# Block 2's mixer in a two-block model kernel: the convolution's projections stand between RWKV's k, r and v, the decayed keys come from the quotients, and scalings move from VectorE to ScalarE

## The chip, the core and the metric

The kernel runs on one core of one Trainium2 chip. The metric is the device time of one execution in microseconds (us). The kernel before takes 2485.76 us, the median of 3 runs (2484.92 to 2486.15).

## The reference

Two blocks run one behind the other, each two layers deep, on 256 tokens of width 1024 in float32. Block 1's layer is an attention mixer and a mixture of experts. Block 2's layer, which the change touches, is a mixer of three branches and a mixture of 32 experts:

```
p = h @ w_in                                  # retention | RWKV | convolution columns
y_ret  = retention(q, k, v, g, ...)
y_rwkv = rwkv7_time_mix(p_rwkv, ...)
y_conv = bgate * conv3(cgate * h_conv)        # three taps along the tokens
merged = sum(gates[i] * (y_i @ w_branch[i]))
x = x + gate1 * (merged @ w_o)
x = x + gate2 * hier_moe(modulate(rms_norm(x)))
```

RWKV's recurrence, for each of 8 heads of width 64 (w the decay, a a sigmoid, kh the normalized key):

```
pf = pf + mu * (prev_token(pf) - pf)          # before r, k, v, w, a, g are cut from it
w  = exp(-exp(-0.5) * sigmoid(w0 + tanh(wd) @ w_lora))
kh = kk * rsqrt(max(sum(kk * kk), 1e-12));  kk = k * k_k
kt = k * (1 + (a - 1) * k_a)
state = state * w - (state @ kh) (a * kh)^T + v kt^T
y     = state @ r
```

## The kernel before, in words

All weights stream from HBM through tiles of 2 MB that SyncE's queue loads in the order in which they are used (`Stream`, `mixer2_tiles`). In the mixer the ring "c" holds three tiles. The ring "x" opens behind the recurrence (`self.st.ring(spare_ring, ...)`), "e" behind retention's transposes (`late_ring()`), and the experts' tiles follow in the same stream as slots come free.

A projection of the mixer (`feat_proj`) makes 128 output columns of all 256 tokens: a chunk. ScalarE casts the weight chunk to `wh` (L240), VectorE makes the rest `wl = w - wh` (L244), each in two buffers, and TensorE does three matmuls for each of 8 row blocks: wh x hi (L249), wh x lo (L250), wl x hi (L251). A tile of weights is four chunks.

`mixer2` writes RWKV's work as straight code: the projections of w and a, then k (`project("k", 4)`), decay and cumulated decay `cum`, the key's norm, r, v, and then the chunk matrices. `shifted` mixes each token with the one before: one ScalarE copy with scale (L581), one VectorE operation (L582), and one for the first token alone (L584). With 64-token chunks, `e = exp(-cum)` divides the keys (`Ki`, `Bi`, the quotients) and `exp(cum)` scales r. `matrices` makes the within-chunk products, `double` inverts them in five levels, and the loop over four chunks `q` runs the recurrence. The keys are also needed as tokens (`toks`, transposed with matmuls, L927), decayed to the chunk's end: `kt * exp(cum_end - cum)` and the same for `a`.

The other branches are a generator, `dense()`: the convolution's three projections (h L639, cgate L644, bgate L656), its gates, its output branch, retention and its gates, and RWKV's output branch. `fill(n)` advances it by n pieces; it stands behind each token transpose, twice in each level of `double` and twice in each `q`, and `fill(1000)` runs the rest.

The text's order is not the order on the engines. With `schedule_with_timeline_sim=True` a planner simulates the program when it is built and puts on each engine the earliest written instruction that is ready by its own costs; on the chip each engine then works in that fixed order. `issue_after` ties an instruction behind another.

Tiles of 4 KB per partition come in tags: "s" with 8 buffers, "d" with 6, "t" with 3. The projections' PSUM tiles (tag "mm") have 4 buffers, the small products' (tag "ch") 2.

Of the kernel before, what the change touches and what calls it, by code (L numbers as in the profile page):

```python
# [10 lines left out]
F32 = mybir.dt.float32  # L11
# [3 lines left out]
AF = mybir.ActivationFunctionType  # L15
OP = mybir.AluOpType
# [92 lines left out]
def mixer2_tiles():  # L109
    cols = lambda *starts: [("w_in_2", (c, c + 512), 4096) for c in starts]  # L110

    def gate(br):
        return ([("w_gate_2", (1024 * br + 512 * c, 1024 * br + 512 * c + 512), 4096) for c in range(2)]
                + [("w_branch_2", br, 4096)])

    return ([("w_in_2", (3584, 3840), 2048)] + cols(2560, 2048, 3072, 3840, 4864, 4352) + gate(2)
            + cols(0, 512, 1024, 1536) + gate(0) + gate(1)
            + [("w_o_2", (512 * c, 512 * c + 512), 4096) for c in range(2)])

# [69 lines left out]
class Kernel:  # L189
# [344 lines left out]
    def mixer2(self, l, prm, mod, cs, nslot, hold, spare, spare_ring, late_ring, gs2, row):  # L534
        nc, tc = self.nc, self.tc
        norm1, mu = (prm[:, P2[n][0]:sum(P2[n])] for n in ("norm1", "mu"))
        cos, sin = cs
        with ExitStack() as ctx:
# [3 lines left out]
            sb = ctx.enter_context(tc.tile_pool(name="m2", bufs=1, reuse_waits="tile"))  # L542
# [35 lines left out]
            def shifted(dst, w, c, mc):  # L578
                p = fproj(w, c)
                m = work.tile([128, 256], F32, name="shm", tag="shm")  # L580
                nc.scalar.activation(m, p, AF.Copy, scale=mu[:, mc:mc + 1])  # L581
                nc.vector.scalar_tensor_tensor(dst[:, 1:], p[:, 1:], mu1[:, mc:mc + 1], m[:, :255], op0=OP.mult,  # L582
                                               op1=OP.add)
                nc.vector.tensor_scalar(dst[:, :1], p[:, :1], mu1[:, mc:mc + 1], None, op0=OP.mult)  # L584

            def head_norm(x, nh, hd, eps, tag):
                xv = x.rearrange("p t (h d) -> p t h d", h=nh)
# [47 lines left out]
            def dense():  # L635
# [13 lines left out]
                w = next_w()  # L649
                for c in range(4):  # L650
                    u = cv_[:, c]
                    nc.vector.tensor_scalar(yc[:, c], u, cvw[:, 2, c:c + 1], None, op0=OP.mult)
                    for i, d in ((1, 1), (0, 2)):
                        nc.vector.scalar_tensor_tensor(yc[:, c, d:], u[:, :256 - d], cvw[:, i, c:c + 1], yc[:, c, d:],
                                                       op0=OP.mult, op1=OP.add)
                    nc.vector.tensor_tensor(yc[:, c], yc[:, c], fproj(w, c), op=OP.mult)  # L656
                    yield
# [85 lines left out]
            def fill(n):  # L743
                for _ in range(n):
                    if gens and next(gens[0], 0) == 0:
                        gens.pop(0)
# [9 lines left out]
            def project(name, m0, tag="s"):  # L756
                dst = feat(name, tag)
                w = next_w()
                for c in range(4):
                    shifted(dst[:, c], w, c, m0 + c)  # L760
                self.st.done()
                return dst

            k_ = project("k", 4)
            wal = pv("wa_lora")
            lw, a_ = xfeat(2), feat("a")
            for c in range(4):
# [8 lines left out]
            with tc.issue_after(self.last_mm.ins):  # L776
# [3 lines left out]
                                     stop=k == 7)  # L780
                nc.vector.tensor_tensor(row, row, pw, op=OP.add)
                nc.vector.tensor_tensor(wr, wr, gs2[:, :, None].to_broadcast([128, 8, 36]), op=OP.mult)
            nc.vector.tensor_scalar(lw, lw, -math.exp(-0.5), None, op0=OP.mult)
            cum = feat("cum")
            for c in range(4):
                nc.vector.tensor_tensor_scan(cum[:, c], smask, lw[:, c], 0.0, op0=OP.mult, op1=OP.add)
            nc.vector.tensor_tensor(lw, cum, lw, op=OP.subtract)
            nc.scalar.activation(lw, lw, AF.Exp)

            kk, sq = feat("kk"), xfeat(3)  # L790
            for c in range(4):
                nc.vector.tensor_scalar(kk[:, c], k_[:, c], pv("k_k")[:, c:c + 1], None, op0=OP.mult)
            nc.scalar.activation(sq, kk, AF.Square)
            pn = ch([128, 2, 8], "pn")
            for t in range(2):
# [4 lines left out]
            nc.vector.tensor_scalar(kn, pn, 1e-12, None, op0=OP.max)  # L800
            kr = carve([128, 2, 8])
            self.rsqrt(sb, kr.rearrange("p t h -> p (t h)"), kn.rearrange("p t h -> p (t h)"), 16)
            for c in range(4):
                nc.vector.tensor_scalar(sq[:, c], a_[:, c], -1.0, pv("k_a")[:, c:c + 1], op0=OP.add, op1=OP.mult)
            nc.vector.scalar_tensor_tensor(k_, sq, 1.0, k_, op0=OP.add, op1=OP.mult)
            kt = k_
            r_ = project("r", 0)
            pk = ch([8, 2, 128], "pk")
            for t in range(2):
                nc.tensor.transpose(pk[:, t], kr[:, t], self.ident)  # L810
            v_ = project("v", 8, "t")
            krT = carve([8, 256])
            nc.vector.tensor_copy(krT, pk.rearrange("p t s -> p (t s)"))
            for c in range(4):
# [10 lines left out]
            for h in range(2):  # L825
                nc.vector.tensor_tensor(KRv[h][:, :, :, 0], by_chunk(kk, h), by_chunk(lw, h), op=OP.mult)
            e = feat("e")
            nc.scalar.activation(e, cum, AF.Exp, scale=-1.0)
            Ki, Bi = feat("Ki"), feat("Bi")
            nc.gpsimd.tensor_tensor(Bi, a_, e, op=OP.mult)  # L830
            nc.vector.tensor_tensor(Ki, kt, e, op=OP.mult)
            e = feat("e")
            nc.scalar.activation(e, cum, AF.Exp)
            for h in range(2):
                nc.vector.tensor_tensor(KRv[h][:, :, :, 1], by_chunk(r_, h), by_chunk(e, h), op=OP.mult)
            for c in range(4):
                nc.vector.scalar_tensor_tensor(r_[:, c], r_[:, c], pv("r_k")[:, c:c + 1], kt[:, c], op0=OP.mult,
                                               op1=OP.mult)
            cl = sb.tile([128, 4, 4], F32, name="cl")
            nc.vector.tensor_copy(cl, cum[:, :, 63::64])  # L840
            cum5 = cum.rearrange("p c (q s) -> p (c q) s", q=4)
            nc.vector.tensor_tensor(cum5, cl.rearrange("p c q -> p (c q)")[:, :, None].to_broadcast([128, 16, 64]), cum5,
                                    op=OP.subtract)
            nc.scalar.activation(cum, cum, AF.Exp)
            lamc = sb.tile([128, 4, 4], F32, name="lamc")
            nc.scalar.activation(lamc, cl, AF.Exp)
            nc.vector.tensor_tensor(kt, kt, cum, op=OP.mult)
            nc.vector.scalar_tensor_tensor(a_, a_, -1.0, cum, op0=OP.mult, op1=OP.mult)
            bon = feat("bon", "t")
            for c in range(4):  # L850
                p = ch([128, 256], "pbon")
# [9 lines left out]
            def matrices(ct):  # L861
                NA[ct], MB[ct] = j8(flat("NA")), j8(xslot(2 + ct))
                xy = tokm("XY")
                X[ct], Y[ct] = j8(xy[:, 0]), j8(xy[:, 1])
                for dst, kind, mask in ((NA[ct], 0, "msn"), (MB[ct], 1, "msk")):
                    for hf in range(2):
                        p = ch([128, 4, 128], "pmat")
                        for c, i in pairs:
                            q = 2 * ct + hf
                            kd = KRv[c // 2][half[i], c % 2, q].rearrange("p k s -> p (k s)")  # L870
                            nc.tensor.matmul(p[half[i], c], lhsT=(Bi, Ki)[kind][half[i], c, 64 * q:64 * q + 64], rhs=kd,
                                             start=True, stop=True)
                        nc.vector.tensor_tensor(dst[:, 4 * hf:4 * hf + 4], p,
                                                cv(mask)[:, None, :].to_broadcast([128, 4, 128]), op=OP.mult)
                p = ch([128, 8, 64], "pmat")
                for hf in range(2):
                    for c, i in pairs:
                        q = 2 * ct + hf
                        nc.tensor.matmul(p[half[i], 4 * hf + c], lhsT=KRv[c // 2][half[i], c % 2, q, 0],
                                         rhs=Bi[half[i], c, 64 * q:64 * q + 64], start=True, stop=True)  # L880
                nc.vector.tensor_tensor(X[ct], p, m8("msl"), op=OP.mult)
                na = NA[ct][:, :, :64]
                nc.vector.scalar_tensor_tensor(Y[ct], na, -1.0, m8("b1t"), op0=OP.mult, op1=OP.mult)
                nc.vector.tensor_tensor(Y[ct], Y[ct], m8("eye"), op=OP.add)
                nc.vector.scalar_tensor_tensor(X[ct], X[ct], -1.0, m8("b1l"), op0=OP.mult, op1=OP.mult)
                nc.vector.tensor_tensor(X[ct], X[ct], m8("eye"), op=OP.add)

            def mm8(p, lhs, rhs):
# [29 lines left out]
            for name, src in (("Vt", v_), ("Kt", kt), ("Bt", a_)):  # L918
                dst = tokp(name)
                toks.append(dst)  # L920
                for t in range(2):
                    p = ch([128, 2, 4, 64], "ptr")
                    for hf in range(2):
                        for c in range(4):
                            q = 2 * t + hf
                            for i in range(2):
                                nc.tensor.matmul(p[half[i], hf, c], lhsT=src[:, c, 64 * q:64 * q + 64],  # L927
                                                 rhs=self.ident[:, half[i]], start=True, stop=True)
                    nc.scalar.copy(dst[:, 2 * t:2 * t + 2], p)
                fill(1)  # L930
            Vt, Kt, Bt = toks

# [928 lines left out]
```

## Time and profile before

| | |
|---|---|
| median of 3 runs | 2485.76 us |
| profiled execution | 2488.0 us, span 2486.2 us |
| TensorE busy | 2031.0 us, 82% of the span |
| VectorE busy | 988.2 us, 40% |
| ScalarE busy | 578.9 us, 23% |
| GpSimd busy | 105.0 us, 4% |
| HBM read | 781.04 MB, 315 GB/s over the span |

Block 2's mixers run from about 854 to 1215 us and from 1672 to 2030 us, its experts behind each of them. In the profile, busy is the time in which an engine had an instruction at work; a row of a group of instructions ends with the idle time before them and what ended it. PEclk is the share of TensorE's full clock that was granted.

### The profile page before, as it was taken

How to read it: one execution, taken by the hardware profiler on the slowest of the kernel's cores; microseconds unless marked ns; L12 is line 12 of the kernel's file. 1: busy time of each engine (PE TensorE's matmuls, PEld its weight loads, DVE VectorE, ACT ScalarE, POOL GpSimd, SP SyncE). 2: the span in 40 equal slices, each digit the busy share in tenths (PEclk: the TensorE clock that was granted, in tenths of full speed). 3: DMA queues.
4: the chain of work that ended last, by engine and by line, in shares of the span. 5: the costliest groups of instructions: out<-in, count | busy, mean ns of one | idle time of the engine just before them, and what ended most of it. 6: DMA issues, size and time to landing. Idle time of an engine off the chain costs nothing. (4 is left out here: it accounts for less than half of the span.)

```text
span 2486.2 us, 46552 instructions
## 1 busy us (share of the span) xinstructions
PE 2031.0 (82%) x20511; PEld 1427.4 (57%) x20511; DVE 988.2 (40%) x2151; ACT 578.9 (23%) x1163; POOL 105.0 (4%) x118
## 2 busy tenths in 40 slices
PE   6998886998878699999886666569999988666665
PEld 5656443756545489989743333338998975333332
DVE  4334333435333576566421111137646653111112
ACT  4332111423111352244310000015224430100000
POOL 0000000001000010001000000001000110000000
PEclk9989998999999899999898888879999989888888
DMA  8576999585999732256699999992216669999997
GB/s 319 233 304 273 423 422 423 201 362 225 406 425 418 291 135 77 89 231 260 261 429 430 428 429 429 429 382 103 103 70 246 243 251 428 429 429 428 429 429 308
DMA packets 65126, 785.24 MB, mean 316 GB/s; under 512 B 8336, under 2 KB 8848, under 8 KB 14480
## 3 DMA queue, kind: packets, MB, share of 16 engines
q1 hardware_dynamic: 63616, 775.00, 75.5%
q10 hardware_dynamic: 1296, 7.11, 0.7%
q8 instruction: 167, 2.74, 0.4%
q14 instruction: 47, 0.39, 0.0%
HBM read 781.04 MB, written 1.05 MB: 315 GB/s over the span
## 5 line engine op out<-in xcount | busy, mean ns | idle before, releaser
L251 PE MATMUL pfeat<-hT,wl 128*128 128x256 f32 x928 | 268.6, 290 | 7.8 <-DVE wl L244 7.8
L249 PE MATMUL pfeat<-hT,wh 128*128 128x256 f32 x928 | 268.9, 290 | 3.3 <-ACT hf L402 1.6
L250 PE MATMUL pfeat<-hT,wh 128*128 128x256 f32 x928 | 265.6, 287 | 0.0
L240 ACT CAST wh<-wc 128x1024 fp32r<-128x1024 f32 x148 | 154.6, 1046 | 350.1 <-PE pfeat L250 240.6
L244 DVE TENSOR_TENSOR wl<-wc,wh 128x1024 fp32r<-128x1024 f32 x148 | 189.0, 1278 | 109.3 <-ACT wh L240 108.9
L1404 DVE TENSOR_TENSOR hs<-hs,pgu 128x128 f32<-128x128 f32 x96 | 27.5, 287 | 491.0 <-ACT hs L1403 490.5
L251 PEld LDWEIGHTS pfeat<-hT,wl 128*128 128x128 f32 x928 | 179.6, 194 | 16.7 <-DVE wl L244 10.0
L1512 DVE TENSOR_TENSOR Y<-pd,gate_row 32x256 f32<-32x256 f32 x256 | 107.6, 420 | 201.3 <-PE pd L1500 198.5
L1403 ACT ACTIVATE hs<-pgu 128x128 f32<-128x128 f32 x96 | 27.0, 281 | 689.9 <-PE pgu L1478 505.6
L249 PEld LDWEIGHTS pfeat<-hT,wh 128*128 128x128 f32 x928 | 179.7, 194 | 11.4 <-issue 3.3
L1390 PE MATMUL pg<-pick,H 128*128 128x128 f32 x1024 | 142.7, 296 | 46.6 <-ACT xg L1398 40.2
L250 PEld LDWEIGHTS pfeat<-hT,wh 128*128 128x128 f32 x928 | 179.6, 194 | 1.4 <-issue 0.7
L1390 PEld LDWEIGHTS pg<-pick,H 128*128 128x128 f32 x1024 | 131.8, 208 | 71.3 <-ACT xg L1398 54.9
L1453 PE MATMUL acc<-Y,P 128*128 128x512 f32 x256 | 129.3, 649 | 21.7 <-DVE Y L1509 15.6
L1509 DVE COPY Y<-pd 32x256 f32<-32x256 f32 x256 | 107.6, 420 | 92.0 <-PE pd L1500 88.8
L1478 PE MATMUL pgu<-wc,xg 128*32 128x256 f32 x1152 | 84.6, 437 | 58.0 <-DMA wc<-in_gu 57.8
L1453 PEld LDWEIGHTS acc<-Y,P 128*128 128x128 f32 x256 | 49.9, 207 | 81.9 <-issue 72.2
L1478 PEld LDWEIGHTS pgu<-wc,xg 128*32 128x32 f32 x1152 | 40.5, 121 | 98.1 <-issue 43.9
L1398 ACT ACTIVATE xg<-pg,mod,gs 128x128 f32<-128x128 f32 x120 | 45.8, 457 | 218.5 <-PE pgu L1478 171.2
L1478 PE MATMUL pgu<-wb,xg 128*32 128x256 f32 x1024 | 70.4, 416 | 22.3 <-DMA wb<-in_gu 22.3
L1472 PE MATMUL pgu<-wa,xg 128*32 128x256 f32 x704 | 80.1, 419 | 6.3 <-DMA wa<-in_gu 6.3
L250 PE MATMUL ptok<-wl,hT 128*128 128x512 f32 (+1 forms) x192 | 78.3, 408 | 1.9 <-DVE wl L289 1.9
(577 smaller groups left out, 3618.2 us busy)
## 6 DMA issues: line engine op xcount, KB each, us to landing
wb<-in_gu SPq DMA_DIRECT2D x54, 2048.0 KB, 29.6
wc<-in_gu SPq DMA_DIRECT2D x50, 2048.0 KB, 28.8
wc<-in_wm SPq DMA_DIRECT2D x36, 2048.0 KB, 8.3
wa<-in_gu SPq DMA_DIRECT2D x20, 2048.0 KB, 16.5
wc<-in_dn SPq DMA_DIRECT2D x16, 2048.0 KB, 38.9
wb<-in_dn SPq DMA_DIRECT2D x16, 2048.0 KB, 38.9
we<-in_gu SPq DMA_DIRECT2D x13, 2048.0 KB, 36.8
wf<-in_gu SPq DMA_DIRECT2D x13, 2048.0 KB, 37.0
```

The costliest lines, as they stand in the source:

```text
L240: nc.scalar.copy(hv, src)
L244: eng.tensor_tensor(lv, src, hv.bitcast(F32), op=OP.subtract)
L249: mm(p, lhsT=lhs[0], rhs=rhs[0], start=first, stop=False)
L250: mm(p, lhsT=lhs[0], rhs=rhs[1], start=False, stop=False)
L251: self.last_mm = mm(p, lhsT=lhs[1], rhs=rhs[0], start=False, stop=last)
L1390: nc.tensor.matmul(p[:, i], lhsT=self.H[:, t, 128 * k:128 * k + 128], rhs=disp[:, t], start=t == 0, stop=t == 1)
L1398: nc.scalar.activation(xg[:, k], p[:, i], AF.Identity, scale=g, bias=b)
L1453: nc.tensor.matmul(acc[2 * t + c], lhsT=P[:, t], rhs=Y[:, 512 * c:512 * c + 512], start=q == 0, stop=q == NE // 4 - 1, skip_group_check=True)
L1472: nc.tensor.matmul(pgu[r:r + 32], lhsT=xg[:, k, 32 * e:32 * e + 32], rhs=gv[ab][:, k, j], start=k == 0, stop=k == 7)
L1478: nc.tensor.matmul(pgu[32 * j:32 * j + 32], lhsT=xg[:, k, 32 * i:32 * i + 32], rhs=gv[k // 4][:, k % 4, j], start=k == 0, stop=k == 7)
L1509: nc.vector.tensor_copy(dst, src)
L1512: nc.vector.tensor_tensor(dst, src, g, op=OP.mult)
```

## The change

The text's order in RWKV's part becomes k, four pieces of `dense` (the convolution's h), w and a, the key's norm, r, four pieces (cgate), v, four pieces (bgate), and the weights are laid out in that order. VectorE's operations with a scale for each partition go to ScalarE: the first token of `shifted`, the convolution's last tap, `kk`, and `(a - 1) * k_a + 1`. The factor `-exp(-0.5)` goes into the exponentials' scale. `Bi = a * e` goes from GpSimd to VectorE. The decayed keys are `Ki * lamc` and `Bi * (-lamc)`, where `lamc` is `exp(cum)` at the chunk's end. One mask of `matrices` goes, and the keys of the last 64 tokens are no longer transposed.

```diff
-    return ([("w_in_2", (3584, 3840), 2048)] + cols(2560, 2048, 3072, 3840, 4864, 4352) + gate(2)
+    return ([("w_in_2", (3584, 3840), 2048)] + cols(2560, 3840, 2048, 4864, 3072, 4352) + gate(2)
...
-                nc.vector.tensor_scalar(dst[:, :1], p[:, :1], mu1[:, mc:mc + 1], None, op0=OP.mult)
+                nc.scalar.activation(dst[:, :1], p[:, :1], AF.Copy, scale=mu1[:, mc:mc + 1])
...
-                    nc.vector.tensor_scalar(yc[:, c], u, cvw[:, 2, c:c + 1], None, op0=OP.mult)
+                    nc.scalar.activation(yc[:, c], u, AF.Copy, scale=cvw[:, 2, c:c + 1])
...
             k_ = project("k", 4)
+            fill(4)
...
-            nc.vector.tensor_scalar(lw, lw, -math.exp(-0.5), None, op0=OP.mult)
+            rate = -math.exp(-0.5)
...
-            nc.scalar.activation(lw, lw, AF.Exp)
+            nc.scalar.activation(lw, lw, AF.Exp, scale=rate)
...
-                nc.vector.tensor_scalar(kk[:, c], k_[:, c], pv("k_k")[:, c:c + 1], None, op0=OP.mult)
+                nc.scalar.activation(kk[:, c], k_[:, c], AF.Copy, scale=pv("k_k")[:, c:c + 1])
...
+            nka = carve([128, 4])
+            nc.vector.tensor_scalar(nka, pv("k_a"), -1.0, 1.0, op0=OP.mult, op1=OP.add)
             for c in range(4):
-                nc.vector.tensor_scalar(sq[:, c], a_[:, c], -1.0, pv("k_a")[:, c:c + 1], op0=OP.add, op1=OP.mult)
-            nc.vector.scalar_tensor_tensor(k_, sq, 1.0, k_, op0=OP.add, op1=OP.mult)
+                nc.scalar.activation(sq[:, c], a_[:, c], AF.Identity, scale=pv("k_a")[:, c:c + 1], bias=nka[:, c:c + 1])
+            nc.vector.tensor_tensor(k_, sq, k_, op=OP.mult)
             kt = k_
             r_ = project("r", 0)
+            fill(4)
...
             v_ = project("v", 8, "t")
+            fill(4)
...
-            nc.gpsimd.tensor_tensor(Bi, a_, e, op=OP.mult)
+            nc.vector.tensor_tensor(Bi, a_, e, op=OP.mult)
...
-            cl = sb.tile([128, 4, 4], F32, name="cl")
-            nc.vector.tensor_copy(cl, cum[:, :, 63::64])
-            cum5 = cum.rearrange("p c (q s) -> p (c q) s", q=4)
-            nc.vector.tensor_tensor(cum5, cl.rearrange("p c q -> p (c q)")[:, :, None].to_broadcast([128, 16, 64]), cum5,
-                                    op=OP.subtract)
-            nc.scalar.activation(cum, cum, AF.Exp)
-            lamc = sb.tile([128, 4, 4], F32, name="lamc")
-            nc.scalar.activation(lamc, cl, AF.Exp)
-            nc.vector.tensor_tensor(kt, kt, cum, op=OP.mult)
-            nc.vector.scalar_tensor_tensor(a_, a_, -1.0, cum, op0=OP.mult, op1=OP.mult)
+            lamc, nlam = (sb.tile([128, 4, 4], F32, name=n) for n in ("lamc", "nlam"))
+            nc.vector.tensor_copy(lamc, e[:, :, 63::64])
+            nc.vector.tensor_scalar(nlam, lamc, -1.0, None, op0=OP.mult)
+            for dst, src, lam in ((kt, Ki, lamc), (a_, Bi, nlam)):
+                dst, src = (x.rearrange("p c (q s) -> p (c q) s", q=4) for x in (dst, src))
+                nc.vector.tensor_tensor(dst, src, lam.rearrange("p c q -> p (c q)")[:, :, None].to_broadcast([128, 16, 64]),
+                                        op=OP.mult)
...
-                nc.vector.tensor_tensor(X[ct], p, m8("msl"), op=OP.mult)
...
-                nc.vector.scalar_tensor_tensor(X[ct], X[ct], -1.0, m8("b1l"), op0=OP.mult, op1=OP.mult)
+                nc.vector.scalar_tensor_tensor(X[ct], p, -1.0, m8("b1l"), op0=OP.mult, op1=OP.mult)
...
-                        for c in range(4):
-                            q = 2 * t + hf
+                        q = 2 * t + hf
+                        for c in range(4 if q < 3 or src is v_ else 0):
...
-                    nc.scalar.copy(dst[:, 2 * t:2 * t + 2], p)
+                    n = 2 if not t or src is v_ else 1
+                    nc.scalar.copy(dst[:, 2 * t:2 * t + n], p[:, :n])
```

## Rows read from the trace of the kernel before

**Rows 1.** Busy time by stretch: start:end, length, engines' busy us, PEclk, DMA share, GB/s.
```profile
885.06:934.05 48.99, 46.09 (x367) 42.24 (x367) 42.22 (x70) 23.90 (x32) 9.06 (x3) 1.00 0.35 130
934.05:1019.96 85.91, 85.91 (x1613) 81.08 (x1612) 53.61 (x79) 20.79 (x27) 0.00 (x0) 1.00 0.21 76
1019.96:1051.00 31.04, 31.04 (x545) 28.90 (x545) 13.78 (x23) 8.03 (x12) 2.08 (x2) 1.00 0.20 70
1190.00:1243.00 53.00, 45.57 (x362) 36.96 (x360) 24.40 (x70) 16.24 (x28) 1.85 (x2) 0.87 0.69 266
1243.00:1675.00 432.00, 290.59 (x3279) 155.25 (x3278) 88.79 (x236) 41.24 (x111) 5.43 (x10) 0.86 1.00 424
2050.00:2486.00 436.00, 289.18 (x3353) 153.62 (x3345) 84.87 (x225) 35.35 (x100) 5.02 (x8) 0.87 0.97 412
```

**Rows 2.** TensorE's matmuls in order of time: start, length, instruction, [idle before <- releaser].
```profile
917.30 0.39 PE L251 MATMUL pfeat<-hT,wl 128*128 128x256 f32 x1 [1.28 <-DVE wl L244]
921.79 0.39 PE L251 MATMUL pfeat<-hT,wl 128*128 128x256 f32 x1 [1.35 <-DVE wl L244]
926.06 0.39 PE L251 MATMUL pfeat<-hT,wl 128*128 128x256 f32 x1 [0.27 <-DVE wl L244]
...
1735.46 0.39 PE L251 MATMUL pfeat<-hT,wl 128*128 128x256 f32 x1 [1.36 <-DVE wl L244]
```

**Rows 3.** VectorE and GpSimd in order of time, around those waits.
```profile
913.32 2.84 POOL L821 TENSOR_TENSOR a<-a,kk 128x1024 f32<-128x1024 f32 x1 [15.91 <-DVE kk L820]
916.24 3.28 POOL L830 TENSOR_TENSOR Bi<-a,e 128x1024 f32<-128x1024 f32 x1
...
913.82 3.43 DVE L244 TENSOR_TENSOR wl<-wc,wh 128x1024 fp32r<-128x1024 f32 x1
917.69 2.90 DVE L831 TENSOR_TENSOR Ki<-k,e 128x1024 f32<-128x1024 f32 x1
```

**Rows 4.** Transposes of the keys, in order of time on TensorE.
```profile
961.29 2.08 PE L927 MATMUL ptr<-core,k 128*64 128x64 f32 x64
```

**Rows 5.** Groups of instructions of 868 to 1051 us: count, busy us, mean ns, idle.
```profile
L584 DVE TENSOR_SCALAR k<-pfeat,mu 128x1 f32<-128x1 f32 x4 | 0.8, 208 | 0.0
L652 DVE TENSOR_SCALAR yc<-cv,par 128x256 f32<-128x256 f32 x4 | 1.4, 351 | 0.1
L783 DVE TENSOR_SCALAR xb<-xb 128x1024 f32<-128x1024 f32 x1 | 0.7, 680 | 0.0
L842 DVE TENSOR_TENSOR cum<-cl,cum 128x1024 f32<-128x1024 f32 x1 | 1.2, 1208 | 0.0
L881 DVE TENSOR_TENSOR XY<-pmat,xa 128x512 f32<-128x512 f32 x2 | 1.4, 688 | 0.0
L581 ACT ACTIVATE shm<-pfeat,prm 128x256 f32<-128x256 f32 x13 | 6.1, 471 | 0.0
```

**Rows 6.** ScalarE in order of time: two casts behind each other, a copy, an Exp, a table.
```profile
897.59 1.05 ACT L240 CAST wh<-wc 128x1024 fp32r<-128x1024 f32 x1 [1.41 <-PE pfeat L250]
900.70 1.05 ACT L240 CAST wh<-wc 128x1024 fp32r<-128x1024 f32 x1 [1.68 <-PE pfeat L250]
...
916.65 0.37 ACT L639 COPY cv<-pfeat 128x256 f32<-128x256 f32 x1
916.92 1.06 ACT L833 ACTIVATE e<-cum 128x1024 f32<-128x1024 f32 x1
...
983.10 1.28 ACT L609 ACT_TABLE_LOAD   x1
```

**Rows 7.** The page's DMA issues: count, size of each, median us to landing.
```profile
wc<-in_wm SPq DMA_DIRECT2D x36, 2048.0 KB, 8.3
```

**Rows 8.** VectorE in order of time: one of the recurrence's copies, retention's first rotation.
```profile
1047.14 0.42 DVE L961 COPY xa<-pu 128x256 f32<-128x256 f32 x1 [0.43 <-PE pu L959]
...
1063.50 0.41 DVE L489 TENSOR_TENSOR rot<-ptok,cos 128x256 f32<-128x256 f32 x1
```

**Rows 9.** TensorE where branch(0) waits for its operand.
```profile
1134.72 0.74 PE L249 MATMUL pbr<-xh,wh 128*128 128x256 f32 x4 [1.89 <-ACT xh L295]
```

More of the change, by code (lines that the diff above doesn't have):

```diff
@@ L827, in mixer2 @@
             e = feat("e")
-            nc.scalar.activation(e, cum, AF.Exp, scale=-1.0)
+            nc.scalar.activation(e, cum, AF.Exp, scale=-rate)
             Ki, Bi = feat("Ki"), feat("Bi")
-            nc.gpsimd.tensor_tensor(Bi, a_, e, op=OP.mult)
+            nc.vector.tensor_tensor(Bi, a_, e, op=OP.mult)
             nc.vector.tensor_tensor(Ki, kt, e, op=OP.mult)
             e = feat("e")
-            nc.scalar.activation(e, cum, AF.Exp)
+            nc.scalar.activation(e, cum, AF.Exp, scale=rate)
             for h in range(2):
```

## The prediction, made before the kernel was run

> **What bounds the kernel now.** I read the busy time by stretch first [rows 1]. Behind each of block 2's mixers come 430 us in which the DMA share is 1.00 or 0.97 at 424 and 412 GB/s while TensorE works 290 us: the experts there go at the pace of their weights. Ahead of the first such stretch, at 1190 to 1243 us, the share is 0.69, so that these loads wait for free tiles, and tiles come free as the mixer ends. A mixer that ends earlier therefore starts the stream earlier, and I pass what it gains to the end one to one.
>
> Inside the mixer the reader is to see TensorE at 85.91 of 85.91 us and 31.04 of 31.04 us in the matrices, the levels and the recurrence, beside VectorE at 53.61 and 13.78 [rows 1]. Only in RWKV's preparation is TensorE short, 46.09 of 48.99 us, where VectorE has 42.22 us of work. The timeline of TensorE names that idle time [rows 2]: three waits for `wl` in each mixer, 1.28, 1.35 and 0.27 us, together 2.90, which is all of 48.99 - 46.09. The row at 1735.46 shows the second mixer's middle one, 1.36. So the mixer is bound by TensorE's own work with 2.9 us of holes, and moving work off VectorE can win those holes at most, unless it shortens TensorE's list.
>
> Why `wl` was late: GpSimd's product of `a` and `kk` runs 913.32 to 916.16 and the VectorE subtraction beside it takes 3.43 us; GpSimd's `Bi` follows to 919.52 and `Ki` beside it takes 2.90 [rows 3]. VectorE's two-input operation of this size takes 1.21 alone [rows 5]. The next `wl` stood behind `Ki`, in the same queue.
>
> **The change part by part, for one mixer.**
>
> Transposes. 16 of the 64 matmuls of `k` go (the last of four chunks), and as many of `a`; 64 take 2.08 us [rows 4], so 2 x 2.08 x 16/64 = 1.04 us less on TensorE, which is saturated there. This term is sure to within the wait that may follow it.
>
> `Bi` to VectorE. GpSimd's 3.28 us go. VectorE gets 1.21 more and `Ki` goes from 2.90 to 1.21, so the pair takes 2.42 instead of 2.90 [rows 3, 5]: nearly as long a block in VectorE's queue ahead of a `wl`. The hole of 1.35 closes only if it stands apart from the critical `wl`; below, that is what the other removals buy. From both sides it is 0 to 1.35; I take 1.35, since in the new order more chunks lie around it. The product of `a` and `kk` stays on GpSimd. Its hole of 1.28 goes or stays with what lies beside it: I take half, 0.64. The third, 0.27, I count as gone.
>
> VectorE's list. It loses 14 first tokens at 0.21 (2.9), twelve scalings of 128x256 at 0.35 (`yc`, `kk`, `sq`: 4.2), the scaling of `lw` 0.68, the subtraction from the chunk's end 1.21, two masks at 0.69 (1.4) and the 1.69 by which `Ki` was stretched; it gains `Bi` 1.21 and two small ones of at most 0.21 [rows 3, 5]. That is 12.1 - 1.6 = 10.5 us of relief, at 86% load before (42.22 of 48.99, rows 1). It is worth nothing by itself where TensorE is full; it makes the holes' closing likely. If VectorE were the bound of the preparation, its 10.5 us could bring no more than the 2.90 anyway.
>
> ScalarE's list. It gains twelve of 0.47 and 14 tiny ones, which no row shows: between 0 and the 0.47 of a full one, near the small end since VectorE's one-column form costs 0.21 against 0.35. It loses one Exp of 1.06 [rows 6] and a tiny one. At 23.90 of 48.99 us [rows 1] it has room for 12 x 0.47 + 14 x 0.21 = 8.6. What waits behind each is the next cast. Casts 3.11 us apart [rows 6], and cast plus subtraction 1.05 + 1.21 = 2.26, leave 0.85 for a chunk; a tiny operation of at most 0.47 fits. I cost it at nothing; with VectorE eating that slack too, 14 x 0.21 = 2.9 would come back, from the other end nothing is gained. The Trainium skill's page "ScalarE: Activation LUTs", in "Rules for kernel authors", wants multiplications on VectorE and not on ScalarE. The rows agree on the direction, 0.47 against 0.35; by that rule the twelve moved ones would cost 12 x 0.12 = 1.4 us a mixer, and the sum would be 2482.1 instead of 2479.2. I don't follow it here because ScalarE doesn't end the chunk.
>
> Waits that are added. Readers of a shifted tile now wait for two engines, and `kk` on ScalarE waits for VectorE's mix of the last chunk of k, with casts queued behind it and TensorE behind those. That cast has idled 1.41 and 1.68 us before it started [rows 6], so 0 is the likely price and two VectorE operations of at most 1.21 each, 2.4, the other end, once a mixer.
>
> Loads. The tiles are the same in number and size, in another order on SyncE's queue. A piece of `dense` gives its tile back only when the next piece begins, so one load is asked for a projection later. Four chunks of 3.11 us make 12.4 us, a load lands in 8.3 [rows 7], and three tiles are there: nothing. Uncovered, one late load would cost some 8.3.
>
> The moved projections. Twelve chunks issue the same matmuls, casts and subtractions earlier. They were the filler beside matrices and levels; now the gates, the convolution's output branch and retention's first projections fill there. The same work on a full TensorE: nothing, if the filler holds out (the slower rival).
>
> The decayed keys from the quotients are two VectorE products as before; they wait for `e`, needed only by the transposes.
>
> Sum: 1.04 + 1.35 + 0.27 + 0.64 = 3.30 us a mixer, 6.6 for two. The profiled execution took 2488.0 us around its span of 2486.2 and would take 2481.4; it stands 2.24 above the median, so the median goes from 2485.76 to **2479.2**. With no hole closed the terms give 2.1, so 2483.7; with all closed 2 x (1.04 + 2.90) = 7.9, so 2477.9.
>
> **The rivals.**
>
> Order doesn't matter. The planner already took projections of the convolution forward: the copy of its first chunk stands on ScalarE at 916.65, ahead of an Exp [rows 6], although its text comes behind the matrices. So the text's new order may change little, `Bi` and `Ki` still block a `wl`, and only the transposes' 2.1 us remain: 2483.7. For it: the pair on VectorE is 2.42 against 2.90. Against it: 10.5 us of relief.
>
> Tables. Gates are Sigmoids. If the planner puts one ahead of the second Exp of `cum`, ScalarE loads tables twice more, 1.28 each [rows 6], and casts wait: at most 2.56 a mixer, 5.1 in all, 2484.3. Against it: v's and bgate's projections, eight chunks, lie ahead of the gates. The Trainium skill, same page, "Table sets: the hidden batching unit", says to batch functions by set; no run here shows yet whether the new order does.
>
> Slower: the filler runs out in the recurrence. With twelve pieces used up early, the 21 pieces that stand in tokens, levels and recurrence reach into retention. Before it, `decay` takes a tile "s", then `yt` and `rq` ask for more, when the matrices, tokens and `XY` hold seven of eight. `rq` can't be written until the second `q` lets a tile go; its projection and that of `rk` hold all four "mm" tiles, and no projection is left to run. Then TensorE idles over VectorE's copies, three of 0.42 in a step [rows 8], so 1.26 us a step and 3.8 for three, and over two rotations of 12 operations at the 0.33 to 0.41 of the first [rows 8], 4.0 each: 11.8 a mixer in full. That makes 2485.8 + 23.5 - 7.9 = 2501, half of it 2490. It decides from 3.9 us a mixer on, where it eats the whole gain. For it: the counts of tiles. Against it: eight units of projection precede the shortage; at about 3 us each (casts 3.11 apart, rows 6) they fill some 24 of the 31.04 us of that stretch [rows 1].
>
> Better still: retention ends earlier and covers the wait of branch(0), 1.89 [rows 9] and about 0.5 behind it, in both mixers: 2477.9 - 4.7 = 2473.2.
>
> **How the numbers follow.** Forecast 0.48, order doesn't matter 0.22, tables 0.06, slower 0.20, better still 0.04. A measurement of this kernel tells some 0.2% from no change, 5 us: faster is below 2480.8, slower above 2490.7. Nearly all of the forecast and the better case, less what lies above 2480.8, make 0.51 faster; three quarters of the slower rival, 0.16 with a remainder, make slower; 0.33 is between. The range 2473 to 2491 leaves out that 0.16 and some 0.02 below. The forecast's own range is 2476 to 2482.
>
> **What would show it.** Right: no VectorE row stretched to 2.9 or 3.4 beside `Bi`, waits for `wl` below 1.3 us in the preparation, two transposes' groups of 48 matmuls near 1.56 us, stretches of full DMA that start 3.3 and 6.6 us earlier and keep their length. Wrong: new waits for `wh` or `wl` in the projections, TensorE below its stretch between 1020 and 1090, more table loads than before ahead of the gates, or a mixer that ends earlier with the experts' stretch longer by as much.

## The result, and the profile after

The changed kernel takes 2521.69 us (median of 4 runs, 2519.45 to 2523.44), the kernel before 2485.34 beside it: ratio 1.0136, 95% interval [1.0118, 1.0154]. It is 36 us slower, where 6.6 us faster were forecast. The profiled execution took 2522.56 us around a span of 2520.8.

All of it lies in block 2's mixers. I take a mixer from ScalarE's first `scaled` to TensorE's `prow`: 331.4 and 333.2 us before, 352.0 and 348.5 after, together 36.0 more. The busy time by stretch of the changed kernel (columns as in [rows 1]):

```profile
885.06:952.45 67.39, 63.06 (x466) 59.51 (x464) 45.35 (x66) 32.22 (x50) 6.16 (x2) 0.92 0.34 126
952.45:1036.00 83.55, 83.55 (x1453) 78.40 (x1452) 47.67 (x64) 22.69 (x30) 0.00 (x0) 1.00 0.30 109
1036.00:1093.00 57.00, 57.00 (x716) 44.80 (x714) 30.57 (x53) 15.21 (x20) 1.24 (x2) 1.00 0.21 75
1139.00:1151.00 12.00, 1.75 (x10) 1.46 (x10) 6.65 (x9) 1.75 (x3) 1.64 (x1) 0.68 0.37 129
1190.00:1243.00 53.00, 44.86 (x277) 39.38 (x276) 33.20 (x70) 20.93 (x30) 7.04 (x10) 0.93 0.68 264
1261.00:1695.00 434.00, 295.23 (x3299) 158.50 (x3294) 89.48 (x239) 41.46 (x111) 5.47 (x10) 0.86 1.00 423
```

Matrices, levels and recurrence are as full as before, and the experts' stretch has its old pace. What is new is a hole of some 10 us at 1139 to 1151, TensorE busy 1.75 of 12.00 us. The second mixer has the same one (1.68 of 12.00 at 1969 to 1981). TensorE in order of time there:

```profile
1139.13 0.49 PE L719 MATMUL pro<-rv,rsc 128*128 128x128 f32 x2 [0.22 <-DVE rsc L708]
...
1150.19 1.09 PE L731 MATMUL pyr<-core,ro 128*128 128x128 f32 x4 [10.12 <-DVE ro L725]
...
1154.20 1.01 PE L249 MATMUL pbr<-xh,wh 128*128 128x256 f32 x3 [1.66 <-ACT xh L295]
```

TensorE has issued retention's last output `pro` and waits for its normalization. VectorE shows the chain. Each step stands behind the one before; three of them wait for a step between, two on ScalarE and one on GpSimd:

```profile
1140.51 1.22 DVE L589 TENSOR_REDUCE hm<-ro 128x8 f32<-128x1024 f32 x1 [1.43 <-ACT ro L722]
...
1141.97 1.22 DVE L591 TENSOR_TENSOR ro<-ro,hm 128x1024 f32<-128x1024 f32 x1
1144.38 1.22 DVE L595 TENSOR_REDUCE hv<-hsq 128x8 f32<-128x1024 f32 x1 [1.18 <-ACT hsq L593]
...
1147.56 1.23 DVE L599 TENSOR_TENSOR ro<-ro,hr 128x1024 f32<-128x1024 f32 x1 [1.75 <-POOL hr L321]
1148.82 1.23 DVE L725 TENSOR_TENSOR ro<-ro,rg 128x1024 f32<-128x1024 f32 x1
```

The chain is no shorter in the kernel before, where it runs from 1115.61 to 1126.68 us (here from 1140.51 to 1150.05). But there TensorE was full meanwhile, with 118 of the 192 projection matmuls of gates(0). The stretch of the kernel before from retention's last `pro` on:

```profile
1114.81:1129.16 14.35, 14.35 (x122) 14.35 (x121) 12.04 (x12) 7.33 (x12) 1.64 (x1) 1.00 0.41 148
```

In the changed kernel all 192 ran from 1104.8 to 1136.2, beside RWKV's tail (`pyT`, `pg`) and ahead of retention's last outputs. Nothing is left to cover the chain. Behind the hole TensorE also works at its lower level of 1.2 GHz: the granted clock is 0.50 from 1151 to 1157 us.

The preparation is not tighter either, and its granted clock is 0.92 where it was 1.00 (first row above and in [rows 1]). TensorE's waits there, first mixer and one of the second, which answer to [rows 2]:

```profile
925.87 0.39 PE L249 MATMUL pfeat<-hT,wh 128*128 128x256 f32 x1 [1.01 <-ACT wh L240]
927.91 0.39 PE L251 MATMUL pfeat<-hT,wl 128*128 128x256 f32 x1 [1.53 <-DVE wl L244]
940.12 0.39 PE L249 MATMUL pfeat<-hT,wh 128*128 128x256 f32 x1 [1.02 <-ACT wh L240]
...
1758.97 0.39 PE L251 MATMUL pfeat<-hT,wl 128*128 128x256 f32 x1 [1.54 <-DVE wl L244]
```

What stands ahead of them on VectorE, and GpSimd's product beside it (answering to [rows 3]):

```profile
920.43 2.90 DVE L831 TENSOR_TENSOR xb<-kk,xb 128x512 f32<-128x512 f32 x1
...
924.37 1.21 DVE L835 TENSOR_TENSOR Bi<-a,e 128x1024 f32<-128x1024 f32 x1
925.51 1.21 DVE L836 TENSOR_TENSOR Ki<-k,e 128x1024 f32<-128x1024 f32 x1
926.64 1.21 DVE L244 TENSOR_TENSOR wl<-wc,wh 128x1024 fp32r<-128x1024 f32 x1
```

```profile
919.52 3.26 POOL L826 TENSOR_TENSOR a<-a,kk 128x1024 f32<-128x1024 f32 x1 [17.84 <-ACT yc L652]
```

`Bi` and `Ki` take 1.21 each, as costed, but the product of `a` and `kk` still stretches what lies beside it, and the pair still stands ahead of a `wl`. The transposes and a first token on ScalarE (a group: count, busy us, mean ns, idle before):

```profile
984.92 1.62 PE L928 MATMUL ptr<-core,k 128*64 128x64 f32 x48
988.93 1.62 PE L928 MATMUL ptr<-core,a 128*64 128x64 f32 x48
```

```profile
L584 ACT ACTIVATE r<-pfeat,mu 128x1 f32<-128x1 f32 x4 | 1.0, 260 | 4.3 <-DVE r L582 4.3
```

### The profile page after: what moved, and what is told of

The parts are those of the page before. It is cut to its first block, busy times and chain, and to the rows that moved or that the text cites. A ratio compares the mean times of both kernels' runs of the same rounds, so it can differ in the third digit from the quotient of the medians.

```text
span 2520.8 us, 46375 instructions
## 1 busy us (share of the span) xinstructions
PE 2047.7 (81%) x20447; PEld 1436.6 (57%) x20447; DVE 977.0 (39%) x2097; ACT 594.1 (24%) x1211; POOL 96.5 (4%) x116
## 5 line engine op out<-in xcount | busy, mean ns | idle before, releaser
L244 DVE TENSOR_TENSOR wl<-wc,wh 128x1024 fp32r<-128x1024 f32 x156 | 194.1, 1245 | 177.2 <-ACT wh L240 173.9
L240 ACT CAST wh<-wc 128x1024 fp32r<-128x1024 f32 x156 | 163.1, 1047 | 324.5 <-PE pfeat L250 166.8
L1480 PE MATMUL pgu<-wc,xg 128*32 128x256 f32 x1088 | 79.4, 434 | 42.2 <-DMA wc<-in_gu 42.1
L1502 PE MATMUL pd<-wc,hs 128*32 128x256 f32 x1024 | 73.8, 420 | 18.1 <-DMA wc<-in_dn 11.3
```

Of the source, the lines that this page charges most:

```text
L240: nc.scalar.copy(hv, src)
L244: eng.tensor_tensor(lv, src, hv.bitcast(F32), op=OP.subtract)
L1480: nc.tensor.matmul(pgu[32 * j:32 * j + 32], lhsT=xg[:, k, 32 * i:32 * i + 32], rhs=gv[k // 4][:, k % 4, j], start=k == 0, stop=k == 7)
L1502: nc.tensor.matmul(pd[32 * jo:32 * jo + 32, ab], lhsT=hT[:, c0:c0 + 32], rhs=dv[:, ab, jj, 256 * jo:256 * jo + 256], start=jj == 0, stop=j ...
```

## The experiments

Theory A: the order is the cause; TensorE's filler is a fixed stock, and what is used in the preparation is missing under retention's normalization. Rival B: the operations moved to ScalarE and VectorE hold up the casts. Rival C: the loss is spread over the mixer, and the hole only shows what would be lost elsewhere. Block 1 ahead of the mixers varies by 10 us from one profile to another (it ends at 844 to 854 us), and all that lies outside the mixers by 14 us (1810.6 to 1824.8 in the kernels of this table), though the edits don't touch it. So I read small effects from the mixers' stretches, summed over both. Each ratio is to the kernel before as measured beside that run (2484.3 to 2486.9 us):

| kernel | time, us | ratio to before, 95% | mixers, us |
|---|---|---|---|
| before | 2485.34 | | 664.6 |
| changed | 2521.69 | 1.0136 [1.0118, 1.0154] | 700.6 |
| e1, order undone | 2479.09 | 0.9980 [0.9968, 0.9993] | 658.2 |
| e2, order alone | 2524.99 | 1.0170 [1.0151, 1.0190] | 709.8 |
| f12, tail later | 2494.61 | 1.0046 [1.0030, 1.0062] | 682.3 |
| d4, fill behind k only | 2508.29 | 1.0106 [1.0085, 1.0126] | 682.0 |
| e1 + Bi on GpSimd | 2482.78 | 0.9995 [0.9979, 1.0011] | 663.6 |
| e1 + a*kk on VectorE | 2481.36 | 0.9985 [0.9970, 1.0000] | 660.6 |
| e1 + first tokens on VectorE | 2478.69 | 0.9963 [0.9940, 0.9985] | 661.0 |
| f12 + a*kk on VectorE | 2494.97 | 1.0033 [1.0018, 1.0047] | 676.6 |

**Order undone, order alone.** e1 takes the order out of the changed kernel; e2 puts it alone into the kernel before.

```diff
-    ... + cols(2560, 3840, 2048, 4864, 3072, 4352) + ...
+    ... + cols(2560, 2048, 3072, 3840, 4864, 4352) + ...
...
-            fill(4)      (three times: behind k, r and v)
```

> The changed kernel with its order undone: the three fills behind k, r and v are gone and the loads stand in the old order; all other edits stay. Theory A (the order is the cause: retention's normalization is left without cover, about 12 us in each mixer, and the rest of the 36 us is what the moved projections themselves cost): the loss is gone and only the small gains are left, 2479 to 2484 us. Rival B (the operations moved to ScalarE and Bi on VectorE hold up the casts of the projections): the loss stays for the most part, 2500 us or more.

> The kernel before with the order alone: three fills and the new order of loads. Theory A: as slow as the changed kernel or a little slower, 2520 to 2526 us, with TensorE idle for 10 us ahead of retention's last transposes in both mixers. Rival B: at most a third of the loss, below 2498 us.

Both went as theory A has it, 2479.1 and 2525.0; B falls. The order costs 42 us with the other edits and 45 without them (mixers' stretches). Its two halves, the fills and the order of the loads, were not tried apart; no engine of the mixers waits for a load by more than 0.3 us in any of these kernels. e2 has the same hole:

```profile
1150.53 1.08 PE L731 MATMUL pyr<-core,ro 128*128 128x128 f32 x4 [10.11 <-DVE ro L725]
```

**Cover for the chain.** The changed kernel with one line more:

```diff
+            fill(12)
             head_norm(yt.rearrange("p (t d) -> p t d", t=2), 8, 64, 64e-5, "s")
```

> The changed kernel with one line more: twelve pieces of the filler are taken between the recurrence and RWKV's normalization, so that retention's transposes, scores and outputs stand ahead of RWKV's closing transposes, and these and five chunks of gates come behind retention's outputs. Theory A: the wait ahead of retention's last transposes, 10.3 us in each mixer and some 12 with the waits around it, goes, 2521.7 - 24 = 2498 us; what is left above the kernel before, 12 us, is the preparation's. Rival C (the loss is the many switches between small groups and projections and the lower clock behind them, spread over the mixer; the wait at its end only shows what TensorE would have lost elsewhere): 2515 us or more.

2494.61: 27 us came back where 24 were expected, but only 18.3 of them lie in the mixers. Most of the rest is block 1's, which is 7 us shorter in this profile and which the line doesn't touch. By the mixers alone the time would be some 2503 us, 5 above A's 2498 and still far below C's 2515: C falls for that half of the loss, and 17.7 us are left. TensorE in the 30 us ahead of the last transposes, then the first of these:

```profile
1103.00:1133.47 30.47, 29.26 (x273) 27.27 (x272) 22.96 (x28) 14.06 (x21) 5.92 (x2) 1.00 0.55 212
```

```profile
1133.47 2.01 PE L731 MATMUL pyr<-core,ro 128*128 128x128 f32 x8
```

They start without a wait: RWKV's closing transposes now run under retention's chain.

**A third of the dose.** Only the fill behind k stays, and cgate and bgate are loaded behind v.

> The changed kernel with one fill of the three, the one behind k. Theory A: the cover behind retention's outputs shrinks with the dose, from five chunks of gates to some two and a half, so that the wait there is about 5 us in a mixer instead of 10, and the time 2490 to 2500 us. If the loss went with the number of moved chunks alone, a third of 36 us, it would be 2497 us, so that the length of the wait in the trace decides here and not the time. Rival B: about the changed kernel's 2521 us.

```profile
1142.11 1.09 PE L731 MATMUL pyr<-core,ro 128*128 128x128 f32 x4 [4.76 <-DVE ro L725]
```

The wait is 4.76, as A has it, for 58 covering matmuls instead of 118. The time, 2508.3, is 8 us above its range: the mixers are 17.4 longer than before, and only some 10 of that are the wait. f12's mixers are as long (682.3) at a time 14 us lower; that difference lies outside the mixers, 1824.8 us here and 1810.6 in f12.

**The chain taken away.** Retention's normalization is left out, in the changed kernel and in the one before. That changes the values that reach the router: the first experts' stretch has 4337 matmuls instead of 3642 and becomes 613 and 608 us instead of 480; so the times (2637.6 and 2602.9) say nothing here, and only the mixers do.

```diff
-                head_norm(ro, 4, 128, 1e-5, "s")
```

> The changed kernel without retention's group normalization (its sums, squares, root and the two products are left out; the product with the gate stays). Theory A (TensorE waits out this chain in both mixers): the wait of 10.3 us ahead of retention's last transposes shrinks to the product with the gate, 1 to 2 us, and the time falls by 2 x 9 to 10, to 2501 to 2504 us. Rival C (the loss is spread over the mixer, and what this chain frees is lost elsewhere): 2515 us or more.

> The control: the kernel before without the same normalization. Theory A: five chunks of gates cover the chain there, so that nothing is won, 2482 to 2486 us. If the chain were on the path there too, it would fall by as much as the changed kernel does, to 2465.

```profile
1142.92 0.66 PE L730 MATMUL pyr<-core,ro 128*128 128x128 f32 x4 [1.72 <-DVE ro L724]
```

The wait shrinks to 1.72. From retention's first `pro` to its last transposes the changed kernel loses 8.4 us in either mixer. But the control is not still: its mixers fall from 664.6 to 657.1, since TensorE's order behind the outputs becomes another one there (first `pro` to last transposes 15.5 instead of 24.4 us, the rest 58.5 instead of 54.0); the changed kernel's fall to 686.0. The place is shown, the sum is not.

**The smaller terms.** On e1, where the order doesn't hide them:

```diff
-            nc.vector.tensor_tensor(Bi, a_, e, op=OP.mult)
+            nc.gpsimd.tensor_tensor(Bi, a_, e, op=OP.mult)
```

> The changed kernel without its order, and with Bi back on GpSimd. By the prediction's terms 1.35 us a mixer come back, the stretch of a mixer goes from 329.0 to 330.3 and the time from 2479.1 to 2481.8. If the move of Bi brought nothing, the stretch stays within 0.4 of 329.0. The stretch decides, since the runs of one kernel lie further apart than 2.7 us.

```diff
-            nc.gpsimd.tensor_tensor(a_, a_, kk, op=OP.mult)
+            nc.vector.tensor_tensor(a_, a_, kk, op=OP.mult)
```

> The changed kernel without its order, and with the product of a and kk on VectorE too, so that GpSimd shares no operation with VectorE in the preparation. Without the order two waits of 1.25 and 0.89 us are left there in each mixer, behind this product. If sharing makes them, they go: the stretch is 327 us and the time 2475. If VectorE's own list makes them (the product adds 1.21 to it), they stay or grow, 329 to 330 us.

TensorE's waits in this place, first mixer, of e1, of `Bi` on GpSimd, and of the product on VectorE:

```profile
909.31 0.39 PE L249 MATMUL pfeat<-hT,wh 128*128 128x256 f32 x1 [1.09 <-ACT wh L240]
910.54 0.38 PE L251 MATMUL pfeat<-hT,wl 128*128 128x256 f32 x1 [0.73 <-DVE wl L244]
```

```profile
920.35 0.58 PE L251 MATMUL pfeat<-hT,wl 128*128 128x256 f32 x1 [3.00 <-DVE wl L244]
```

```profile
915.18 0.39 PE L249 MATMUL pfeat<-hT,wh 128*128 128x256 f32 x1 [0.83 <-ACT wh L240]
```

So GpSimd's products make more than half of these waits. Sharing with VectorE is one way in which they can; the other is that a product takes longer on GpSimd while `Bi` waits for it. The product of `a` and `kk` and then `Bi`, in e1 and with the product on VectorE:

```profile
902.89 3.26 POOL L823 TENSOR_TENSOR a<-a,kk 128x1024 f32<-128x1024 f32 x1 [13.38 <-ACT shm L581]
907.01 1.21 DVE L832 TENSOR_TENSOR Bi<-a,e 128x1024 f32<-128x1024 f32 x1
```

```profile
909.91 1.22 DVE L823 TENSOR_TENSOR a<-a,kk 128x1024 f32<-128x1024 f32 x1
912.04 1.22 DVE L832 TENSOR_TENSOR Bi<-a,e 128x1024 f32<-128x1024 f32 x1
```

`Bi` starts 4.12 us behind the product's start in the first and 2.13 in the second. In e1 it could not have started before the product's end at 906.15 even without sharing, so that by this estimate sharing is 0.86 of the 1.99 us and the slower product the rest. No run tells the two apart.

From the first low-rank product to the first matrix, `Bi` on VectorE is worth 0.8 and 0.7 us in the two mixers, not 1.35. The whole mixers, by which this was to be read, grow by more with `Bi` on GpSimd, by 2.5 and 2.9 us, but 1.5 of each is TensorE's clock at their end (last section). `a` times `kk` on VectorE is worth another 2.4 and 1.1; the first has 1.3 us of clock in it (granted 0.58 in the 4 us behind e1's waits in its first mixer, 1.00 in its second). This gain did not reach the time (2481.4 against 2479.1): the clock behind branch(0) takes 1.5 us back in the first mixer, and in the second the changed order behind it costs 2.6 us ahead of the last transposes.

> The changed kernel without its order, and with the fourteen first tokens of the shifted tiles back on VectorE. The prediction costed their move to ScalarE at nothing, with 2.9 us a mixer as the other end. If it is nothing, the stretch from the first low-rank product to the first matrix stays at 60 to 61.5 us; if ScalarE's queue held up casts by it, 58 us or less; if VectorE needs the relief, 62 us and more.

The stretch is 57.8 us, which by the text above means a hold-up by ScalarE's queue; but 24 matmuls of the next projection (457 against 433 on TensorE, 2.9 us at 0.12) had moved out of it. With them it is 60.7 and lies within the two 61.4 and 60.1 of e1, and the time is the same: nothing, as costed.

> The changed kernel with RWKV's tail put later (as in f12) and the product of a and kk on VectorE. TensorE's order is that of f12, so the difference of the two lies in the preparation alone. With the moved projections there, TensorE waits 1.17, 1.69 and 1.18 us in a mixer, behind the 3.3 us in which GpSimd multiplies and a VectorE operation beside it is stretched. If sharing makes these waits, at least 2.5 of the 4.0 us go, in each mixer, and the stretches of the mixers sum to 677 instead of 682.3 us. If the moved projections alone make them (more casts and subtractions beside the same chain), they stay: 682 us.

The sum, 676.6, is what was expected, but only in part for the reason given: the waits fell only from 1.01, 1.54 and 1.02 to 0.82, 0.66 and 1.02. The preparation won 5.0 us in the first mixer and 1.6 in the second. Compared matmul by matmul, the place around these waits won 2.0 and 3.2, in part by the shorter waits and in part because the clock no longer falls behind them (granted 0.57 and 0.50 in f12 in the 4 us behind the second wait, 1.00 in both mixers here). The rest is the clock at another place ahead of them (last section), which gave 3.0 us in the first mixer and took 1.5 in the second. The time did not move (2494.97 against 2494.61).

## Why the prediction was wrong

**The step that failed** is "The moved projections": "The same work on a full TensorE: nothing, if the filler holds out". It cost 42 us in the two mixers. The filler is a stock. The planner had put some of these chunks into the preparation already, so that the order moves five more, net, ahead of the first matrix (576 `pfeat` matmuls instead of 458, 24 to a chunk). They let RWKV end later (`pyT` starts 256.5 us into the first mixer instead of 212.4), while `dense` kept using up pieces beside it. Whichever chain ends last then has none.

**The slower rival** had the mechanism, but the wrong place. Its price, 11.8 us a mixer, was for tiles in the recurrence, and gave 2501 in full, 20 us short of the measured time; TensorE is full there (57.00 of 57.00). The shortage came one chain later, at 10.1 us plus 0.55 of waits ahead of it. I counted which pieces would be used up and asked who goes hungry next, but not who goes hungry last. The row to read was the kernel before's 14.35 us at 1114.81: a serial chain over three engines whose whole cover was projections. f12 shows that one line of the text's order is enough to cover it again.

**The other half**, 17.7 us over the kernel before that f12 keeps, is in small pieces. In the second mixer f12 is 11.5 us longer than e1. From each TensorE matmul to the next, summed by tile: `pfeat` 3.5 more (half of it longer waits in the preparation, 3.6 instead of 1.8 us), `ptok` 2.4 (it now alternates with the recurrence's small matmuls), `pg` 1.8 (waits for `yw`), `pbr` 1.1, `pyr` 0.8, the rest about 2. In the first mixer it is 12.6 us longer, and 2.6 of these are the clock behind small matmuls (last section). Why these pieces cost more is read from the traces and not shown by a run; which could be had back was not tried beyond the product of `a` and `kk`.

**Terms that held.** The transposes: three groups take 5.11 instead of 6.04 us in a mixer, 0.93 for 1.04. The loads: 8.6 us to landing, no wait. First tokens: 0.26 us each, nothing lost. The twelve scalings take 0.51 to 0.59 us on ScalarE instead of 0.47; their move was not undone alone, so whether it costs anything is open. **Tables:** a single load ahead of the three Exps, as before, so that rival did not occur.

**Terms that were off.** The holes: e1 keeps 1.09 + 0.73 of 2.90, so 1.08 was won and not 2.26, `Bi`'s part being 0.7 to 0.8. The waits I took for closed stand behind the product of `a` and `kk`, which stayed on GpSimd. e1's 2479.09 meets the forecast's 2479.2 partly by chance: transposes and holes make 2.0 us a mixer, and 1.2 to 1.5 come from the clock behind branch(0) (last section), both read in one profile, whose time, 2471.68, is the lowest of e1's twelve.

e1, the change without its order, lies 0.2% below the kernel before (interval 0.9968 to 0.9993); with the first tokens on VectorE it can't be told from that.

## What to carry to other kernels

Independent work that fills a full engine is a stock to be spent on serial chains: before moving a piece of it earlier, list all chains behind it to the end of the stage, with their lengths and what covers each, and look at the last one first. "The engine is full anyway" prices a move at nothing only if every later chain keeps its cover. After a change of order compare stretches with equal work in them; a boundary between two interleaved streams moves by itself.

## What the runs showed that was not expected

TensorE's clock falls in stretches without an idle gap. Window, length, PE, PEld, DVE, ACT, POOL, granted clock, DMA share, GB/s, for the 28 projection matmuls behind 32 small ones (`pshift`, `pn`) in the first mixer; f12, then f12 with the product on VectorE, whose order on TensorE is the same there:

```profile
891.12:897.01 5.89, 5.89 (x28) 5.89 (x29) 1.40 (x2) 1.73 (x4) 2.90 (x1) 0.50 0.02 8
```

```profile
895.08:898.39 3.31, 3.31 (x29) 3.31 (x29) 1.40 (x2) 1.87 (x5) 2.88 (x1) 1.00 0.12 45
```

Both are busy all the time, the first at TensorE's lower level of 1.2 GHz (0.50), the second at 2.4. The same order gives both, so chance has a part in it. But of the six kernels with the fill behind k, the clock falls here in 8 of 12 mixers, for 1.5 to 2.6 us each, and of the six without it in none of 12. So it is a part of the order's price, and not luck alone. With that fill TensorE's last wait of over 0.3 us stands 6 to 10 us ahead of this place, without it 24 us; whether that is what tips it was not tried.

Likewise in the 8 us behind branch(0)'s wait of some 2 us the clock is 1.00 in both mixers of e1 and falls in both with `Bi` on GpSimd; in the kernel before it is 0.79 in both, and with the first tokens on VectorE 1.00 in one and 0.79 in the other. First mixer of e1, then with `Bi` on GpSimd:

```profile
1129.00:1137.00 8.00, 8.00 (x69) 8.00 (x69) 5.24 (x8) 3.00 (x3) 3.51 (x5) 1.00 1.01 428
```

```profile
1139.00:1147.00 8.00, 8.00 (x57) 8.00 (x57) 3.97 (x6) 2.10 (x2) 2.91 (x4) 0.81 1.01 426
```

That is 1.5 us of a mixer, as much as most of the terms argued about. What tips it stays open.

Beside GpSimd's product (919.52 to 922.78) VectorE's L831 takes 2.90 us and ends at 923.33; its other half takes 0.69 alone, and 922.78 + 0.69 is 923.47. So it did next to nothing until GpSimd was done. The rows of the kernel before agree: `Ki` ends at 920.59, and `Bi`'s end plus 1.21 is 920.73 [rows 3]. The Trainium skill, "SBUF — State Buffer", in "Terms", says that VectorE and GpSimd lock a shared port pair for a whole instruction and that the loser waits; the trace agrees, 2.90 against 0.69.
